# A 2x2-block form in seven products for the FFN's second matrix product, with operands passed through DRAM

## The chip, the cores and the metric

The kernel runs on one core of one Trainium2 chip. The time is the device time of one execution in microseconds; a kernel's time is the median of its runs. Engines are named as in the profile: PE (TensorE, matrix products; PEld loads its weights), DVE (VectorE), ACT (ScalarE), POOL (GpSimd), and SP (SyncE), which issues the transfers here. Each engine works through its own queue in order.

## The reference

One step of a two-layer encoder with 1024 prompt tokens and 64 sample tokens, all taken together as T = 1088 columns. Layer 0 is a Mamba-2 mixer and an FFN, layer 1 is a chunk-band attention and an FFN. What matters here is the FFN and what stands around it:

```python
def swiglu(u, w_in, w_out):
    g, up = jnp.split(u @ w_in, 2, axis=-1)
    return (jax.nn.silu(g) * up) @ w_out
...
        xp = xp + rmsnorm(mp, nw[1])
        xs = xs + rmsnorm(ms, nw[1])
        xp = xp + rmsnorm(swiglu(rmsnorm(xp, nw[2]), ffn_w_in[layer], ffn_w_out[layer]), nw[3])
        xs = xs + rmsnorm(swiglu(rmsnorm(xs, nw[2]), ffn_w_in[layer], ffn_w_out[layer]), nw[3])
```

D_MODEL is 1024 and the hidden width is 2816, which is 22 blocks of 128. All of it is float32. The two layers' FFNs have weights of their own.

## The kernel before

Activations lie transposed, features on the 128 partitions and tokens along the free dimension. A float32 product is computed in three passes of fp32r operands: every operand v is split into a high part (a copy on ACT, written as fp32r) and a low part (v minus the high part, on DVE), and a tile of the output sums high x high, high x low and low x high. A "split" below means this pair of instructions. For weights it is `Weights.part` (L302 on ACT, L303 on DVE).

The FFN's first product (`run_pair`, L1224 to L1277, matmuls L1240 to L1242 into `px`) already works on 2x2 blocks: the weights and the normed input are cut in halves along both of their axes, and seven products of block sums (`PRODS`, L330) stand in place of eight. It runs over pairs of hidden blocks t and over two token halves, b = 0 (512 tokens, two quarters of 256) and b = 1 (576 tokens, two quarters of 288). Five pairs of b = 0 are computed plainly (`plain_pairs`). Each gated hidden block is stored to DRAM (`hscr`).

The FFN's second product (L1396 to L1430, matmuls L1410 to L1412 into `po`) is plain. Three token slices (`SL`: 384, 384 and 320 columns) are the outermost loop, then 8 output tiles m, then 22 hidden blocks k, three passes each: 1584 matmuls in a layer. A task `loader` (L1291) reads the hidden blocks of a slice back from DRAM into staging tiles (`sg`) and splits them (L1303, L1304). Weights come by SP into a ring of two raw tiles (`raw`), are split into a ring of three (`hl`), and are read anew for every slice: 72 parts of 1024 or 768 columns in a layer. An output tile is copied out of PSUM by ACT; ACT squares it and POOL adds up the squares (L444).

After a slice, the task `end` norms it: `rb_steps` reduces the sums of squares over the partitions by tiny matmuls (`nst`, L451), makes the reciprocal root by ten small DVE operations (`nv`, L457 to L468), spreads it on a diagonal (`dg`, L472) and broadcasts it by a matmul (`nbp`, L480), which ACT copies to `rb` (L484). Then DVE and POOL scale the slice and add the residual (L1331, L1332). In layer 0, `end` also makes the operands of attention from the slice: splits (L1351, L1352), sums of squares (L1356, L1357), and a second `rb_steps`. Attention's weights are scaled while they are split (L312, L315), and its first products run as `unit`s (L418 to L420).

What sets the order is a recording layer. The Python code runs through the work for PE; tasks (`loader`, `end`) are generators that are spawned and take their turns when the PE stream's time (an estimate that `st.run` advances) passes the delays they yield, or when the stream waits for something that they provide (`st.wait_for`). A priority (`tc.high_priority`) moves single instructions ahead on their queue. The delays are constants at the top (`EP_W`, `ER_W`, `EQ_W`, `RB_WAIT`).

## Time and profile before

| what | us |
|---|---|
| median of 3 runs | 3074.6 (3072.13 to 3075.79) |
| profiled execution, its own time | 3078.88 |
| its span | 3077.2 |
| first products (matmuls into `px`), layers 0 and 1 | 943.0 to 1364.5, 2373.0 to 2794.8 |
| second products (matmuls into `po`), layers 0 and 1 | 1364.5 to 1636.9, 2794.8 to 3059.7 |
| hand-over to attention after layer 0's second product | from 1636.9 |
| end of the kernel after layer 1's second product | 3059.7 to 3077.2 |

In the profile, L12 is line 12 of the kernel. A window's row gives the busy time of every engine in a stretch, with the count of instructions, the granted TensorE clock, the share of the DMA engines and the rate. A group's row gives the instructions of one line and shape: count, total busy us, mean ns of one, and the idle time that its engine had just before them, with what ended most of it. A timeline's row begins with start and duration; in brackets stands the idle time before it and what ended that.

### The profile page before, as it was taken

How to read it: one execution, taken by the hardware profiler on the slowest of the kernel's cores; microseconds unless marked ns; L12 is line 12 of the kernel's file. 1: busy time of each engine (PE TensorE's matmuls, PEld its weight loads, DVE VectorE, ACT ScalarE, POOL GpSimd, SP SyncE). 2: the span in 40 equal slices, each digit the busy share in tenths (PEclk: the TensorE clock that was granted, in tenths of full speed). 3: DMA queues.
4: the chain of work that ended last, by engine and by line, in shares of the span. 5: the costliest groups of instructions: out<-in, count | busy, mean ns of one | idle time of the engine just before them, and what ended most of it. 6: DMA issues, size and time to landing. Idle time of an engine off the chain costs nothing. (4 is left out here: it accounts for less than half of the span.)

```text
span 3077.2 us, 57007 instructions
## 1 busy us (share of the span) xinstructions
PE 2974.8 (97%) x21665; PEld 2908.0 (95%) x21665; DVE 2120.1 (69%) x4582; ACT 1422.8 (46%) x2599; POOL 844.3 (27%) x969
## 2 busy tenths in 40 slices
PE   8999999999999999999999999999898999999998
PEld 8899999999999999999999899999898999999997
DVE  8988888885878544674576777767578645575544
ACT  6655555554543322344455655555553322244432
POOL 1334343421343334331231000000153334342112
PEclk9999999999999999999999999999998999999999
DMA  3333233334443222355563222222344222246654
GB/s 118 119 86 110 87 108 88 109 119 149 147 152 92 75 81 78 102 165 171 177 199 120 85 63 63 69 64 83 121 140 131 79 78 79 76 122 183 205 182 132
DMA packets 200419, 354.36 MB, mean 115 GB/s; under 512 B 21104, under 2 KB 150192, under 8 KB 200144
## 3 DMA queue, kind: packets, MB, share of 16 engines
q1 hardware_dynamic: 200080, 350.64, 37.2%
q8 instruction: 170, 2.79, 0.4%
q14 instruction: 105, 0.86, 0.1%
q0 software_dynamic: 64, 0.07, 0.0%
HBM read 283.30 MB, written 62.87 MB: 112 GB/s over the span
## 5 line engine op out<-in xcount | busy, mean ns | idle before, releaser
L418 PE MATMUL mm<-r,hl 128*128 128x384 f32 (+2 forms) x1632 | 549.0, 336 | 7.0 <-ACT r L1717 6.3
L303 DVE TENSOR_TENSOR hl<-raw,hl 128x1024 fp32r<-128x1024 f32 (+1 forms) x276 | 337.5, 1224 | 307.3 <-ACT hl L302 306.2
L420 PE MATMUL mm<-r,hl 128*128 128x384 f32 (+2 forms) x1632 | 530.5, 325 | 3.6 <-DVE hl L315 2.8
L419 PE MATMUL mm<-r,hl 128*128 128x384 f32 (+2 forms) x1632 | 529.7, 325 | 0.7 <-DVE r L1718 0.7
L302 ACT CAST hl<-raw 128x1024 fp32r<-128x1024 f32 (+1 forms) x276 | 279.2, 1012 | 277.9 <-DMA raw<-in_w_f_dram 99.8
L1241 PE MATMUL px<-r,hl 128*128 128x288 f32 (+1 forms) x1192 | 350.0, 294 | 0.0
L444 POOL TENSOR_TENSOR ssum<-ssum,sq 128x256 f32<-128x256 f32 (+3 forms) x153 | 171.1, 1120 | 576.4 <-ACT sq L443 572.9
L418 PEld LDWEIGHTS mm<-r,hl 128*128 128x128 f32 x1632 | 311.7, 191 | 8.9 <-ACT r L1717 6.5
L420 PEld LDWEIGHTS mm<-r,hl 128*128 128x128 f32 x1632 | 310.4, 190 | 5.3 <-DVE hl L315 4.2
L1240 PE MATMUL px<-r,hl 128*128 128x288 f32 x1056 | 311.2, 295 | 4.3 <-DVE u L1255 4.3
L419 PEld LDWEIGHTS mm<-r,hl 128*128 128x128 f32 x1632 | 311.6, 191 | 1.4 <-DVE r L1718 1.0
L1242 PE MATMUL px<-r,hl 128*128 128x288 f32 x1056 | 310.9, 294 | 0.0
L1242 PE MATMUL px<-rx,hl 128*128 128x256 f32 x816 | 229.2, 281 | 7.1 <-DVE hl L303 7.1
L1240 PE MATMUL px<-rx,hl 128*128 128x256 f32 x816 | 229.9, 282 | 0.1
L1241 PEld LDWEIGHTS px<-r,hl 128*128 128x128 f32 x1192 | 224.0, 188 | 0.1
L1411 PE MATMUL po<-rx,hl 128*128 128x384 f32 (+1 forms) x640 | 207.6, 324 | 0.0
L1240 PEld LDWEIGHTS px<-r,hl 128*128 128x128 f32 x1056 | 198.6, 188 | 5.4 <-DVE u L1255 5.4
L1410 PE MATMUL po<-rx,hl 128*128 128x384 f32 (+1 forms) x608 | 199.1, 327 | 0.0
L1242 PEld LDWEIGHTS px<-r,hl 128*128 128x128 f32 x1056 | 198.4, 188 | 0.0
L1412 PE MATMUL po<-rx,hl 128*128 128x384 f32 (+1 forms) x608 | 197.3, 325 | 0.2 <-DVE hl L303 0.2
L1241 PE MATMUL px<-rx,hl 128*128 128x256 f32 x680 | 190.7, 280 | 0.0
L260 POOL TENSOR_TENSOR tt<-raw 128x512 f32<-128x512 f32 x44 | 60.2, 1369 | 398.7 <-DMA raw<-in_w_f_dram 301.9
(337 smaller groups left out, 8187.9 us busy)
## 6 DMA issues: line engine op xcount, KB each, us to landing
raw<-in_w_f_dram SPq DMA_DIRECT2D x204, 512.0 KB, 3.7
raw<-in_w_in_dram SPq DMA_DIRECT2D x40, 512.0 KB, 3.7
raw<-in_w_f_dram SPq DMA_DIRECT2D x48, 384.0 KB, 3.2
sg<-hscr SPq DMA_DIRECT2D x88, 192.0 KB, 3.6
raw<-in_w_so_dram SPq DMA_DIRECT2D x32, 512.0 KB, 3.9
dm<-acd SPq DMA_DIRECT2D x64, 192.0 KB, 3.8
raw<-in_w_kv_dram SPq DMA_DIRECT2D x18, 512.0 KB, 3.7
raw<-in_w_o_dram SPq DMA_DIRECT2D x16, 512.0 KB, 3.8
```

The source lines that it names most:

```text
L302: self.nc.scalar.copy(h, v)
L303: (eng or self.eng or self.nc.vector).tensor_tensor(lo, v, h, op=ALU.subtract)
L418: PE.matmul(ps[:, :n], h_, xh, start=(first and i == 0), stop=False)
L419: PE.matmul(ps[:, :n], h_, xl, start=False, stop=False)
L420: PE.matmul(ps[:, :n], l_, xh, start=False, stop=(last and i == nk - 1))
L444: (eng or G).tensor_tensor(ssum[:, :n], ssum[:, :n], q[:, :n], op=ALU.add)
L1240: PE.matmul(ps, wh, ah[:, k, :], start=(k == 0), stop=False)
L1241: PE.matmul(ps, wh, al[:, k, :], start=False, stop=False)
L1242: PE.matmul(ps, wl, ah[:, k, :], start=False, stop=(k == 3))
L1410: PE.matmul(ps[:, :n], wh, xh, start=(k == 0), stop=False)
L1411: PE.matmul(ps[:, :n], wh, xl, start=False, stop=False)
L1412: PE.matmul(ps[:, :n], wl, xh, start=False, stop=(k == FT - 1))
```

## The change

The second product is cut as the first one: output tiles in two halves (4 tiles j each), hidden blocks in even and odd ones (11 pairs k), tokens in the two quarters of each half b. Seven products take the place of eight. The loop over products (`PHASES`) is outermost: P1, P6, P2, P7 and P5 for both halves b, then P4 and P3 for b = 0, then P4 and P3 for b = 1. Each product of a half takes 4 x 11 x 3 matmuls of 256 or 288 columns, 1848 in a layer. Its weights come in parts of 768 and 640 columns (`KIT`), read once for both halves in the shared phases and once for each half in the last four.

- The seven operands of a pair k (two of the four hidden blocks' own rows, a11 and so on, and four sums, s1 to s4) are formed in the first product (`Hidden.row`, `Hidden.sums`): four sums on DVE for each pair and half, and a store of every operand to a DRAM scratch `hop`. The first blocks of a pair wait for their partner in a lent tile of the ring R, in a stage tile, or in their own tile.
- The four weight sums (`Hidden.weights`) are formed in the first product too: 16 rounds, one in 17 of the stream's us, each with four loads into stage tiles behind a tiny POOL copy, four sums on DVE and four stores to the scratch `wt`.
- The order of the first product's pairs (`RUN`) begins with pair 5 and then has pair 4 for b = 1 alone, and ends with four pairs of b = 1 alone, where five stood at the end before.
- `loader` brings the operands back and splits them, 154 tiles of 256 or 288 columns in place of 66 of 384 or 320.
- A product is not copied out but added on DVE to accumulators (L1612), 56 additions in a layer in place of 24 copies on ACT (the first product's 8 are still copies). The additions follow the Winograd form.
- `end` runs for four quarters instead of three slices. In layer 0 quarters are put together to attention's slices (`PIECES`, L1501, with sums of squares L1506 on POOL or DVE into `tot0`, `tot1`).
- Weights may take a third raw tile, lent by the ring R. Attention's evacuations `evq` and `evv` wait for the slice's `rb`.

The core of the diff:

```diff
+WT_GAP = 17.0
...
-EP_W, ER_W, EQ_W = (9.4, 9.4, 5.0), (8.9, 8.9, 4.5), (11.0, 11.0, 11.0)
+EP_W, ER_W, EQ_W = (5.0, 5.0), (7.0, 7.0), (6.0, 6.0)
...
+KH = FT // 2
+FH = KH * P
+KORD = [*range(5, KH), *range(5)]
+KIT = (0, 6), (6, 5)
+WCH = (0, 3), (3, 3), (6, 3), (9, 2)
+RUN = [(5, (0, 1)), (4, (1,))] + [(t, (0, 1)) for t in range(6, FT)] + [(t, (1,)) for t in range(4)]
...
+PHASES = [(p_, (0, 1)) for p_ in (P1, P6, P2, P7, P5)] + [(P4, (0,)), (P3, (0,)), (P4, (1,)), (P3, (1,))]
...
-    hd_ = [dr.tile([P, FT, T], F32, name=f"hscr{i}") for i in range(2)]
+    hop_ = [dr.tile([P, 7, KH, T // 2], F32, name=f"hop{i}") for i in range(2)]
+    wt_ = [dr.tile([P, 4, 4, FH], F32, name=f"wt{i}") for i in range(2)]
...
-        for s in range(NSL):
-            for m in range(KD):
-                for k0, nk in KCH:
-                    W.plan(dict(src=[w2[m][:, k0 * P:(k0 + nk) * P]], n=nk * P))
+        for p_, _ in PHASES:
+            for j in range(4):
+                for k0, nk in KIT:
+                    if p_ in (P1, P2, P3):
+                        v = half(w2[j + 4 * (p_ == P3)], p_ != P1, k0, nk)
+                    else:
+                        v = wt[:, j, {P6: WT2, P7: WT3, P5: WT1, P4: WT4}[p_], k0 * P:(k0 + nk) * P]
+                    W.plan(dict(src=[v], n=nk * P, lend=1))
...
+        def sums(self, b, t_, c, u_):
+
+            if self.first(b, t_):
+                return
+            F, S = self.held[b, 0], self.held[b, 1]
+            q = nsb.tile([P, 384], F32, tag="sq", bufs=2, name="hs")[:, :BN[b] // 2]
+            if t_ % 2:
+                (a21, a11, a22, a12), (s3, s1, s2, s4) = (F, S, c, u_), (S, F, q, u_)
+            else:
+                (a22, a12, a21, a11), (s3, s1, s2, s4) = (F, S, c, u_), (q, c, F, S)
+            for i, d, x_, y_, op in (
+                ("s3", s3, a11, a21, ALU.subtract), ("s1", s1, a21, a22, ALU.add),
+                ("s2", s2, a22, s3, ALU.subtract), ("s4", s4, a12, s2, ALU.subtract),
+            ):
+                V.tensor_tensor(d, x_, y_, op=op)
+                self.store(b, t_, OPI[i], d)
+            self.ok.add((b, KORD.index(t_ // 2)))
...
+        def weights(self):
+
+            w2, wt = w_f2[self.layer], wt_[self.layer]
+            for j in range(4):
+                for k0, nk in WCH:
+                    b22, b12, b11, b21 = (stage[0]()[:, :nk * P] for _ in range(4))
+                    G.tensor_copy(b22[:, 0:1], self.held[1, 0][:, 0:1])
+                    for t_, m, h in ((b22, j + 4, 1), (b12, j + 4, 0), (b11, j, 0), (b21, j, 1)):
+                        nc.sync.dma_start(blocks(t_), half(w2[m], h, k0, nk))
+                    for i, d, x_, y_, op in (
+                        (WT3, b22, b22, b12, ALU.subtract), (WT1, b12, b12, b11, ALU.subtract),
+                        (WT2, b11, b22, b11, ALU.add), (WT4, b21, b21, b11, ALU.subtract),
+                    ):
+                        V.tensor_tensor(d, x_, y_, op=op)
+                        nc.sync.dma_start(wt[:, j, i, k0 * P:(k0 + nk) * P], d)
+                    yield 0, WT_GAP
...
+                    d = hid.out(b, t_, 0, x["c22"])
+                    G.tensor_tensor(d, x["p1"], x["u2"], op=ALU.mult)
+                    hid.row(b, t_, 0, d)
+            if p_ == P3:
+                hid.sums(b, t_, x["c22"], x["u3"])
...
+                        yield 0, 0, lambda: (b, k) in hid.ok and sh.room((b, k, 0), (b, k, 1))
+                        h_, l_ = (rr(sh.get((b, k, part))) for part in range(2))
+                        n = BN[b] // 2
                         t_ = stage[0]()[:, :n]
                         with tc.high_priority(LDP):
-                            nc.sync.dma_start(t_, hd[:, k, o:o + n])
+                            nc.sync.dma_start(t_, hid.hop[:, OPN[p_], k, b * 256:b * 256 + n])
                             A.copy(h_, t_)
                             V.tensor_tensor(l_, t_, h_, op=ALU.subtract)
...
+                    yq = ys[qq]
+                    for m in range(KD):
+                        uh, ul = u[s][m]
+                        ym, ss_ = yq[m // 4][:, m % 4, c:c + w_], tot[s][:, a:a + w_]
+                        with tc.high_priority(ENP[last]):
+                            A.copy(uh[:, a:a + w_], ym)
+                            V.tensor_tensor(ul[:, a:a + w_], ym, uh[:, a:a + w_], op=ALU.subtract)
+                        if m == 0:
+                            A.activation(ss_, ym, AF.Square)
+                        else:
+                            A.activation(ym, ym, AF.Square)
+                            (V if last and m % 2 else G).tensor_tensor(ss_, ss_, ym, op=ALU.add)
+                        yield 0, ES[last]
...
+                if q:
+                    s = q - 1
+                    done2.append(s)
+                    yield 0, EQ_W[last]
+                    yield from rb_steps(tot[s], SL[s][1], [], ER_W[last], rb_out[s])
+                    done2.append(("rb", s))
...
+                for i, (t_, bs) in enumerate(RUN):
+                    ends = ((0,) if t_ == FT - 1 else ()) + ((1,) if i == len(RUN) - 1 else ())
+                    run_pair(t_, W.get(), bs, ends, ops, hid, px, tmp, i == 0)
+                    if i == 3:
+                        st.spawn(hid.weights())
...
+            for p_, bs in PHASES:
+                for j in range(4):
+                    ps = {b: px.tile([P, 512], F32, tag="mm", name="po") for b in bs}
+                    for k0, nk in KIT:
                         w = W.get()
                         h, v = w["w"]
+                        for b in bs:
+                            n = BN[b] // 2
+                            for k in range(k0, k0 + nk):
+                                st.wait_for(lambda: (p_, b, k) in hl)
+                                xh, xl, sh = hl[p_, b, k]
+                                a = (k - k0) * P
+                                wh, wl = h[:, a:a + P], v[:, a:a + P]
+                                PE.matmul(ps[b][:, :n], wh, xh, start=(k == 0), stop=False)
+                                PE.matmul(ps[b][:, :n], wh, xl, start=False, stop=False)
+                                PE.matmul(ps[b][:, :n], wl, xh, start=False, stop=(k == KH - 1))
...
+                            if p_ == P1:
+                                A.copy(at("p1"), pb_)
+                            else:
+                                for d, x_ in {
+                                    P6: (("u2", "p1"),), P2: (("p1", "p1"),), P7: (("u3", "u2"),),
+                                    P5: (("c22", "u3"), ("u2", "u2")), P4: (("u3", "u3"),), P3: (("u2", "u2"),),
+                                }[p_]:
+                                    V.tensor_tensor(at(d), pb_, at(x_), op=ALU.add)
...
+                if len(bs) == 1:
+                    b = bs[0]
+                    q = 2 * b + (p_ == P3)
+                    ys[q] = (acc["p1", b], acc["u2", b]) if p_ == P3 else (acc["u3", b], acc["c22", b])
+                    st.spawn(end(q, ys[q], ss[q], more))
...
         def evq(j):
             def f(s, p_):
                 n = SL[s][1]
+                st.wait_for(lambda: ("rb", s) in done)
```

Lines move by the change: `nst` L451 to L501, `nv` L457 to L507 and following, `dg` L472 to L522, `nbp` L480 to L530, the units L418 to L468, weight splits L303 to L349 and L315 to L361, the norm steps L1331 and L1332 to L1478 and L1479, attention's splits L1352 to L1501.

PE at the hand-over from layer 0's second product to attention, before, behind the last slice: the reduction `nst` of the last slice's norm stands among units (`mm`) of attention.

```order
L419 MATMUL mm<-r,hl 128x384
L420 MATMUL mm<-r,hl 128x384
L451 MATMUL nst<-ones,ssum 128x1 x3
L418 MATMUL mm<-r,hl 128x384
L419 MATMUL mm<-r,hl 128x384
```

The broadcast `nbp` that belongs to it stands 32 rows later, again among units:

```order
L418 MATMUL mm<-r,hl 128x384
L419 MATMUL mm<-r,hl 128x384
L420 MATMUL mm<-r,hl 128x384
L480 MATMUL nbp<-dg,frac 128x320
L418 MATMUL mm<-r,hl 128x384
```

PE at the same place now, 24 units behind the last product; `tot` holds the sums for attention's first slice, `ssum` those of a quarter's own norm.

```order
L469 MATMUL mm<-r,hl 128x384
L470 MATMUL mm<-r,hl 128x384
L501 MATMUL nst<-ones,tot_16708 128x1 x3
L501 MATMUL nst<-ones,ssum 128x1 x3
L530 MATMUL nbp<-dg,frac 128x384
L468 MATMUL mm<-r,hl 128x384
L469 MATMUL mm<-r,hl 128x384
```

Two reductions and a broadcast that stood apart, with units between them, stand in direct succession.

DVE at the same place, before: behind the last weight splits of the second product (L303) come attention's weights (L315), an evacuation of attention (`vt`) and the small operations of the norm.

```order
L303 TENSOR_TENSOR hl<-raw,hl 128x1024 x2
L303 TENSOR_TENSOR hl<-raw,hl 128x768
L303 TENSOR_TENSOR hl<-raw,hl 128x1024 x2
L303 TENSOR_TENSOR hl<-raw,hl 128x768
L315 SCALAR_TENSOR_TENSOR hl<-raw,pcs,hl 128x128 x24
L1568 TENSOR_TENSOR vt<-mm,rbf 128x384
L457 TENSOR_SCALAR nv<-nst 128x3
L458 TENSOR_SCALAR nv<-nv 128x3
L461 TENSOR_TENSOR nv<-nv 128x3
L466 TENSOR_TENSOR nv<-nv 128x3
L467 SCALAR_TENSOR_TENSOR nv<-nv 128x3
L468 SCALAR_TENSOR_TENSOR nv<-nv 128x3
```

DVE now: the first row is the last addition out of PSUM (L1612); `u` and `c` are accumulators, the latter of a quarter that is being normed.

```order
L1612 TENSOR_TENSOR u_17313<-po,u_17313 128x288
L1479 TENSOR_TENSOR c_18583<-c_18583,r 128x288
L361 SCALAR_TENSOR_TENSOR hl<-raw,pcs,hl 128x128 x12
L1478 SCALAR_TENSOR_TENSOR c_18583<-c_18583,pcs,rb 128x288
L507 TENSOR_SCALAR nv<-nst 128x3 x2
L508 TENSOR_SCALAR nv<-nv 128x3
L1478 SCALAR_TENSOR_TENSOR c_18583<-c_18583,pcs,rb 128x288
L511 TENSOR_TENSOR nv<-nv 128x3
L508 TENSOR_SCALAR nv<-nv 128x3
L1479 TENSOR_TENSOR c_18583<-c_18583,r 128x288
L516 TENSOR_TENSOR nv<-nv 128x3
L511 TENSOR_TENSOR nv<-nv 128x3
```

The small operations of two norms (`x2`) now stand behind attention's weights and among the last norm steps of a quarter.

DVE within the second product, before, where the second slice is normed (L1331, L1332) while weights for the third one are split (L303):

```order
L1331 SCALAR_TENSOR_TENSOR y<-y,pcs,rb 128x384 x2
L1332 TENSOR_TENSOR y<-y,rx 128x384
L1331 SCALAR_TENSOR_TENSOR y<-y,pcs,rb 128x384 x2
L1332 TENSOR_TENSOR y<-y,r 128x384
L1331 SCALAR_TENSOR_TENSOR y<-y,pcs,rb 128x384
L303 TENSOR_TENSOR hl<-raw,hl 128x1024
L1332 TENSOR_TENSOR y<-y,r 128x384
L1331 SCALAR_TENSOR_TENSOR y<-y,pcs,rb 128x384 x3
L1332 TENSOR_TENSOR y<-y,r 128x384
L303 TENSOR_TENSOR hl<-raw,hl 128x1024
L1352 TENSOR_TENSOR r<-y,r 128x384 x3
L303 TENSOR_TENSOR hl<-raw,hl 128x768
```

DVE now, in the last two products of layer 0 (b = 1), where the first half's quarters are normed (L1478, L1479) and split for attention (L1501):

```order
L349 TENSOR_TENSOR hl<-raw,hl 128x768
L1479 TENSOR_TENSOR r<-r 128x256
L1478 SCALAR_TENSOR_TENSOR r<-r,pcs,rb 128x256
L1478 SCALAR_TENSOR_TENSOR c_18578<-c_18578,pcs,rb 128x256 x2
L1479 TENSOR_TENSOR c_18578<-c_18578,r 128x256
L349 TENSOR_TENSOR hl<-r,hl 128x640
L1612 TENSOR_TENSOR u_18152<-po,u_18152 128x288
L1478 SCALAR_TENSOR_TENSOR c_18578<-c_18578,pcs,rb 128x256 x2
L1479 TENSOR_TENSOR c_18578<-c_18578,r 128x256
L507 TENSOR_SCALAR nv<-nst 128x2
L1501 TENSOR_TENSOR r<-r 128x256
L508 TENSOR_SCALAR nv<-nv 128x2
```

Splits stood among norm steps before as well; now additions out of PSUM (L1612) and the small operations of a norm stand among them too, and four quarters are worked off within the last four products.

300 lines of the change are left out of this document (191 added, 109 removed).

## Prediction

> **What bounds the kernel now.** I read the busy shares first, then windows over the four long stretches of the two FFNs.
>
> ```profile
> span 3077.2 us, 57007 instructions
> PE 2974.8 (97%) x21665; PEld 2908.0 (95%) x21665; DVE 2120.1 (69%) x4582; ACT 1422.8 (46%) x2599; POOL 844.3 (27%) x969
> core 0: us, PE busy (x) PEld busy (x) DVE busy (x) ACT busy (x) POOL busy (x), PEclk, DMA share, GB/s
> 1364.50:1636.90 272.40, 268.58 (x1619) 266.45 (x1618) 150.40 (x213) 123.95 (x211) 56.13 (x47) 0.99 0.60 184
> 2794.80:3059.70 264.90, 264.34 (x1604) 263.04 (x1602) 124.99 (x160) 105.14 (x162) 39.18 (x32) 1.00 0.59 183
> 943.00:1364.50 421.50, 415.28 (x3279) 414.39 (x3278) 260.58 (x420) 144.12 (x235) 168.39 (x139) 0.99 0.30 93
> 1300.00:1364.00 64.00, 61.92 (x466) 61.23 (x465) 55.77 (x80) 30.55 (x51) 32.25 (x24) 1.00 0.47 146
> 2600.00:2700.00 100.00, 100.00 (x805) 100.00 (x805) 51.09 (x91) 28.43 (x47) 40.10 (x35) 1.00 0.27 81
> 1450.00:1500.00 50.00, 50.00 (x289) 49.51 (x288) 38.45 (x55) 25.93 (x47) 14.64 (x12) 1.00 0.72 232
> 1480.00:1490.00 10.00, 10.00 (x60) 10.00 (x59) 10.00 (x13) 5.16 (x10) 6.24 (x6) 1.00 0.64 207
> ```
>
> PE is busy for 97% of the span. The first two windows are the second products of layers 0 and 1, the third is layer 0's first product. In all of them PE has almost no idle time, so a product costs its matmuls times their pitch. The pitch follows the width: at 384 columns it is 50/289 = 0.173 us (1450 to 1500), and in the first product, which alternates 256 and 288 columns, 100/805 = 0.1243 us (2600 to 2700). Fewer and narrower matmuls are therefore paid in full, as long as operands arrive. The profiled execution took 3078.9 us (span 3077.2 and 1.7 around it), 4.3 above the median of 3074.6. I sum against 3078.9 and take 4.3 off at the end.
>
> **What goes.** Now 3 slices x 8 tiles x 22 blocks x 3 passes = 1584 matmuls per layer; afterwards 7 products x 2 halves x 4 tiles x 11 blocks x 3 passes = 1848, of 256 and 288 columns, the mix of the first product: 1848 x 0.1243 = 229.7 us. Against the two windows that saves 272.4 - 229.7 = 42.7 us in layer 0 and 264.9 - 229.7 = 35.2 in layer 1, together **77.9 us**. Layer 0's window holds stalls, and the matmuls behind them run slower:
>
> ```profile
> 1593.97 0.41 PE L1410 MATMUL po<-r,hl 128*128 128x320 f32 x1 [2.60 <-ACT hl L302]
> 1596.45 0.47 PE L1410 MATMUL po<-rx,hl 128*128 128x320 f32 x1
> 1596.72 0.47 PE L1411 MATMUL po<-rx,hl 128*128 128x320 f32 x1
> 1667.75 2.41 PE L451 MATMUL nst<-ones,ssum 128*128 128x1 f32 x10 [4.84 <-POOL ssum L1357]
> 3059.16 0.31 PE L1411 MATMUL po<-rx,hl 128*128 128x320 f32 x1
> 3059.31 0.31 PE L1412 MATMUL po<-rx,hl 128*128 128x320 f32 x1
> 3060.14 1.28 PE L451 MATMUL nst<-ones,ssum 128*128 128x1 f32 x10 [0.41 <-ACT ssum L1421]
> 3061.46 0.16 DVE L457 TENSOR_SCALAR nv<-nst 128x3 f32<-128x3 f32 x1 [0.77 <-PE nst L451]
> 3061.65 0.17 DVE L458 TENSOR_SCALAR nv<-nv 128x3 int32<-128x3 int32 x1
> 3063.42 0.56 DVE L472 TENSOR_TENSOR dg<-ident,nr 128x384 f32<-128x384 f32 x1
> 3064.04 1.44 PE L480 MATMUL nbp<-dg,frac 128*128 128x320 f32 x2 [2.62 <-DVE dg L472]
> ```
>
> After the wait of 2.60 us the pitch is 0.27 us (1596.45 to 1596.72) where 320 columns else take 0.15 (3059.16 to 3059.31, rounded). Ten or so such matmuls cost some 1.5 us, which I add to every longer stall.
>
> **What comes: DVE.** Durations by shape, from layer 0's second product to the end (x, total, mean ns):
>
> ```profile
> L303 DVE TENSOR_TENSOR hl<-raw,hl 128x1024 fp32r<-128x1024 f32 x135 | 172.3, 1277 | 194.0 <-ACT hl L302 193.6
> L303 DVE TENSOR_TENSOR hl<-raw,hl 128x768 fp32r<-128x768 f32 x48 | 48.9, 1020 | 57.6 <-ACT hl L302 57.6
> L315 DVE SCALAR_TENSOR_TENSOR hl<-raw,pcs,hl 128x128 fp32r<-128x128 f32 x208 | 65.7, 355 | 5.8 <-ACT hl L312 5.5
> L1331 DVE SCALAR_TENSOR_TENSOR y<-y,pcs,rb 128x384 f32<-128x384 f32 x32 | 27.2, 890 | 0.5 <-ACT rb L484 0.5
> L1304 DVE TENSOR_TENSOR r<-sg,r 128x384 fp32r<-128x384 f32 x33 | 20.4, 645 | 9.7 <-ACT r L1303 9.6
> L1352 DVE TENSOR_TENSOR r<-y,r 128x384 fp32r<-128x384 f32 x16 | 15.3, 1000 | 1.0 <-ACT r L1351 1.0
> L1173 DVE SCALAR_TENSOR_TENSOR rx<-rx,pcs,rb 128x256 f32<-128x256 f32 x16 | 11.2, 751 | 0.0
> L1185 DVE SCALAR_TENSOR_TENSOR rx<-rx,pcs,rb 128x256 f32<-128x256 f32 x16 | 7.9, 528 | 1.8 <-ACT rb L484 1.8
> L1267 DVE TENSOR_TENSOR u<-px,u 128x288 f32<-128x288 f32 x23 | 10.4, 452 | 7.3 <-PE px L1242 7.3
> L1332 DVE TENSOR_TENSOR y<-y,r 128x384 f32<-128x384 f32 x14 | 7.7, 548 | 0.0
> L444 POOL TENSOR_TENSOR ssum<-ssum,sq 128x256 f32<-128x256 f32 x28 | 29.1, 1042 | 45.2 <-ACT sq L443 44.3
> L444 POOL TENSOR_TENSOR ssum<-ssum,sq 128x288 f32<-128x288 f32 x28 | 27.4, 981 | 20.4 <-ACT sq L443 19.3
> L1273 POOL TENSOR_TENSOR c<-p,u 128x256 f32<-128x256 f32 x17 | 13.8, 810 | 0.2 <-POOL u L1269 0.2
> ```
>
> *First product.* Each layer gets 11 x 2 x 4 = 88 operand sums of 256 or 288 columns and 64 weight sums of 256 or 384. At L1332's 548 ns for 384 columns (1.43 ns a column) that is 34 + 32 us, with 152 stores and 64 loads on SP. DVE rises from 260.6 to some 327 of 421.5 us, 78%, and PE covers it: PE ran without idle in window 2600 to 2700 with DVE at 51% and POOL at 40%. Were the cover gone, all 66 us would be late. What is dense already is the end: 55.8 of 64 us (1300 to 1364). I take **2 us** a layer, with 0 and 10 as ends: ten single-half sums of about 0.4 us in the last runs, twice over.
>
> *Shared phases* (five products for both halves, 1320 x 0.1243 = 164 us of PE). DVE gets 110 operand splits (272 columns on average, at L1304's 645/384 = 1.68 ns: 50 us), 40 weight splits (20 of 768 at 1.02, 20 of 640 at about 0.87: 38) and 40 evacuations that are now sums (L1267, about 0.44: 18): 106 of 164 us. PE covers that but for waits like the 2.60 above: **2 us** a layer (0 to 5).
>
> *Layer 0's last two phases*, where each half's output is normed and handed to attention while weights are still split. The last excerpt in the section on the change shows splits (L349) queued behind norm steps (L1478) on DVE's one queue. PE needs 264 matmuls x 0.133 us (288 columns) = 35.1 us here. DVE, counted in the order between the last evacuation of P3's first half and the last of all: 14 splits, 7 of 768 and 7 of 640 columns, 7 x 1.02 + 7 x 0.87 = 13.2 (640 lies between the rows); 8 evacuations at 0.45 = 3.6; L1478, 14 of 256 and 5 of 288, 10.3 by L1185's row to 14.9 by L1173's, 12.6; L1479, 10, 4.1; L1501, 4096 columns in 24 pieces, 6.9 by L1304's to 10.7 by L1352's, 9; two chains of small operations and `dg`, 5; four of L315's kind, 1.4. Sum **49 us** against 35.1, so weights come 14 us late, less 2 for what is queued last and no weight needs: **12**, with 6 and 18 as ends (the low and high rows of L1478 and L1501).
>
> *Hand-over to attention.* PE's excerpt of the changed order shows `nst` and `nbp` with nothing between, and only 24 unit matmuls (24 x 0.173 = 4.2 us) after the last product; before, 30 stood between. Behind the last evacuation DVE holds 20 small operations at a pitch of 0.2 (4.0), 20 of L361 (L315 before) at 0.355 (7.1), two `dg` (1.1) and norm steps (some 3): 15 us, so PE waits 15 - 4 = 11, and 2 more for the slow clock: **13**, with 4 (the unhindered chain, 3060.14 to 3064.04) and 17 as ends. Two further `nst`/`nbp` pairs cost about one unhindered chain less the units between, **3 + 3** (1 to 5 each). The old stall of 4.84 goes: **-4.8**. Slow matmuls after two waits for weights: **3**.
>
> *Layer 1's end.* Nothing is handed on there; counted in the same way, DVE has about 27 of 35 us; its tail is as before (288 columns instead of 320), with one evacuation more ahead of the square. **3 us** (0 to 5).
>
> Layer 0: 42.7 - (2 + 2 + 12 + 13 + 6 - 4.8 + 3) = 9.5. Layer 1: 35.2 - (2 + 2 + 3) = 28.2. Sum 37.7: 3078.9 - 37.7 = 3041.2, and 4.3 off: **3037 us** (own range 3020 to 3056).
>
> **Rivals.** *B: the chains hide.* Only unhindered chains remain: 4 + 2 + 2 - 4.8 + 1.6, first product and shared phases 4, tail 0.5, nothing else: 9.3 of 77.9 lost, 3010 less 4.3, **3006**. For it: ACT idles half of the time, and weights have a third raw buffer. Against: 49 us in 35.
>
> *C: DMA sets the pace of the single phases.*
>
> ```profile
> raw<-in_w_f_dram SPq DMA_DIRECT2D x204, 512.0 KB, 3.7
> raw<-in_w_f_dram SPq DMA_DIRECT2D x48, 384.0 KB, 3.2
> sg<-hscr SPq DMA_DIRECT2D x88, 192.0 KB, 3.6
> ```
>
> In the last 66 us I count 11.5 MB of weights, 2 of operands, 3.3 of the residual and 2.1 of stores, 18.9 MB. The busiest row above moved 232 GB/s at a share of 0.72; at 232 it takes 81 us, 15 late per layer, at 232/0.72 = 322 it takes 59 and fits. In place of 12 and 3 the loss is up to 27 and 18 or some 22 more in all: **3059**.
>
> *R: VectorE and GpSimd take turns in layer 0's last two phases.* L1352 took 1000 ns beside GpSimd work where L1304, the same shape, took 645. POOL has 17 operations of 256 columns there at 0.81, 11 of 288 at 0.98 and 14 of 128 at about 0.4, 30 us. If turns were complete, DVE's 49 without PSUM reads and small operations (40) and these 30 make 70 us, late by 35 in place of 14: **3058**. Against it stands the dense row, 10.00 of DVE and 6.24 of POOL in 10 us, unless an instruction that waits for its turn is recorded as busy. The Trainium skill, SBUF — State Buffer, section "Who interferes with whom", states this as a rule: a VectorE instruction with two SBUF inputs and a GpSimd one that reads SBUF exclude each other for a whole instruction. By that page the sum would be 3058; the rows show slowing of that kind, and can't tell waiting from work.
>
> *D: slower, the first product.* If DVE and POOL took turns there, 260.6 + 66 + 168.4 = 495 us of work would stand in 421.5, 73 a layer: 3037 + 146 = **3183**. It decides from 19 us a layer on, which eats the 37.7. For it: today's 260.6 + 168.4 already fill the 421.5. Against: 55.8 and 32.3 busy in 64 us, 138%, with PE at 97%.
>
> *E: the change doesn't do what it says*, the pitch not falling with the width: at 0.15, as for 320 columns now, 1848 of them take 277 us, the gain turns into a loss of 5 + 12, and with the costs of 40: 3078.9 + 17 + 40 - 4.3 = **3132**, slower. The first product's row at the same widths speaks against.
>
> **How the numbers follow.** Chances: forecast 0.48, B 0.20, C 0.12, R 0.10, D 0.07, E 0.03. The range 3003 to 3066 holds B, the forecast's own range and the prices of C and R. What a measurement of this kernel can tell from no change is about 0.2%, 6 us. D and E are slower, 0.10. Of C and R, whose prices lie 15 below the old time, 0.05 falls within 0.2%. Faster: 0.85.
>
> **What would show it.** Right: the second products near 230 us plus stalls, in layer 0 waits on `hl` L348/L349 in the last 35 us, and one long wait on `dg` L522 behind L1777's products. B would show no wait over 4 us there; C waits on `raw` from DMA at a share near 1; R doubled L1501 and L1478; D idle PE between first-product matmuls. Wrong: waits elsewhere, or a first product over 430 us.

## The result, and the profile after

The changed kernel takes 3216.6 us (median, 3216.0 to 3220.3), the kernel before 3075.2 in the same session: ratio 1.0461 (95% interval 1.0443 to 1.048). It is slower by some 141 us, where 38 less were forecast.

The page's head and the windows over the four FFN products of the changed kernel, first products first, then four stretches inside the second products: one of layer 0's shared phases, layer 0's last two phases (P4 and P3 of b = 1), layer 1's P3 of b = 0, and layer 1's last two phases:

```profile
span 3214.5 us, 60252 instructions
PE 2976.2 (93%) x22195; PEld 2892.4 (90%) x22195; DVE 2338.4 (73%) x5248; ACT 1439.4 (45%) x2810; POOL 868.2 (27%) x1041
...
core 0: us, PE busy (x) PEld busy (x) DVE busy (x) ACT busy (x) POOL busy (x), PEclk, DMA share, GB/s
942.80:1442.10 499.30, 444.28 (x3280) 435.94 (x3279) 330.29 (x563) 137.64 (x236) 176.86 (x156) 0.95 0.45 139
2446.70:2942.60 495.90, 441.93 (x3280) 434.43 (x3279) 326.74 (x558) 137.40 (x234) 174.26 (x155) 0.94 0.45 140
1442.00:1692.00 250.00, 239.41 (x1871) 235.98 (x1870) 172.43 (x345) 130.54 (x297) 52.17 (x61) 0.99 0.69 202
2942.40:3192.20 249.80, 238.95 (x1872) 236.12 (x1870) 164.65 (x326) 116.75 (x243) 37.54 (x41) 0.99 0.69 202
...
1500.00:1550.00 50.00, 50.00 (x403) 50.00 (x402) 28.65 (x60) 23.91 (x52) 2.32 (x4) 1.00 0.63 179
1642.60:1692.00 49.40, 41.21 (x282) 38.83 (x281) 49.16 (x97) 29.48 (x81) 34.56 (x41) 0.97 0.69 215
...
3130.80:3149.60 18.80, 17.13 (x140) 16.28 (x139) 11.64 (x24) 8.09 (x14) 4.90 (x6) 1.00 1.01 308
3149.60:3192.20 42.60, 38.30 (x282) 37.21 (x280) 38.53 (x74) 15.27 (x27) 19.69 (x22) 1.00 0.68 205
```

The second products are shorter, as meant. The time is lost where the operands are formed: layer 0's first product grew from 421.5 to 499.3 us with the same matmuls. Idle time of PE in it rose from 6.2 (421.50 - 415.28) to 55.0 us, and the busy time by another 29.0 (444.28 against 415.28): 48.8 + 29.0 = 77.8. Some 21 of the 29.0 go with the granted clock, which is 0.95 over 499.3 us where it was 0.99 over 421.5 (25.0 - 4.2); the rest wasn't traced. By stage, with the forecast's terms beside it (first to last matmul of each stage, from the timelines):

| stage | before | after | difference | forecast |
|---|---|---|---|---|
| first product, layer 0 | 421.5 | 499.3 | +77.8 | +2 |
| first product, layer 1 | 421.5 | 495.9 | +74.4 | +2 |
| second product, layer 0 | 272.5 | 250.1 | -22.4 | -42.7 + 2 + 12 + 3 = -25.7 |
| second product, layer 1 | 264.8 | 249.8 | -15.0 | -35.2 + 2 + 3 = -30.2, with the end |
| from there to layer 1's first product, all of attention | 736.5 | 754.7 | +18.2 | 13 + 6 - 4.8 = +14.2 |
| after the last product | 17.5 | 22.3 | +4.8 | in the 3 above |
| the rest, rounding included | | | -0.5 | 0 |
| span | 3077.2 | 3214.5 | +137.3 | -37.7 |

What PE and DVE waited for there: groups by line and shape in layer 0's first product, of the kernel before and of the changed one. The last part of a row is the engine's idle time just ahead of the group and what ended it.

```profile
L1255 DVE TENSOR_TENSOR u<-px,p 128x288 f32<-128x288 f32 (+1 forms) x39 | 17.2, 440 | 66.1 <-PE px L1242 65.3 <-ACT p L1252 0.8
...
L1257 DVE TENSOR_TENSOR p<-px,p 128x288 f32<-128x288 f32 (+1 forms) x39 | 17.2, 442 | 28.5 <-PE px L1242 28.1
```

```profile
L1377 PE MATMUL px<-r,hl 128*128 128x288 f32 x528 | 162.8, 308 | 43.3 <-DVE u L1392 33.9 <-DVE p L1394 9.1 <-DVE u L1410 0.3
...
L1326 DVE TENSOR_TENSOR sg<-sg 128x384 f32<-128x384 f32 (+1 forms) x64 | 34.1, 533 | 70.3 <-DMA sg<-in_w_f_dram 69.7
...
L324 DVE TENSOR_TENSOR tt<-tt,raw 128x512 f32<-128x512 f32 x21 | 17.8, 846 | 27.3 <-POOL tt L306 27.3
L1305 DVE TENSOR_TENSOR r<-r 128x288 f32<-128x288 f32 (+1 forms) x18 | 16.7, 926 | 22.0 <-POOL r L1412 19.9 <-DMA hop<-r 2.2
L1305 DVE TENSOR_TENSOR r<-r,c 128x288 f32<-128x288 f32 (+1 forms) x17 | 16.1, 949 | 12.7 <-POOL c L1412 12.7
...
L1392 DVE TENSOR_TENSOR u<-px,p 128x288 f32<-128x288 f32 (+1 forms) x39 | 16.2, 434 | 0.0
L1394 DVE TENSOR_TENSOR p<-px,p 128x288 f32<-128x288 f32 (+1 forms) x39 | 16.8, 436 | 3.4 <-PE px L1379 3.0
```

Before, DVE's evacuations waited for PE: 65.3 and 28.1 us ahead of two of their lines. Now they wait for nothing, and PE waits for them. DVE's waits moved to the added sums: the weight sums (L1326) stood 69.7 us for their loads, and the two groups of operand sums (L1305) shown 32.6 us for GpSimd's gated product (L1412). L324, the first product's own block sums of weights, waited 27.3 us for GpSimd's part of them (L306); before it was 18.4. The timeline of the changed kernel at the end of one pair shows how a wait of DVE becomes one of PE:

```profile
1314.57 0.47 POOL L1319 COPY sg<-r 128x1 f32<-128x1 f32 x1
1315.07 1.98 SPq L1321 DMA_DIRECT2D sg<-in_w_f_dram  x4
...
1312.33 1.51 DVE L1305 TENSOR_TENSOR r<-r 128x256 f32<-128x256 f32 x1 [1.53 <-POOL r L1412]
1314.54 0.46 DVE L1305 TENSOR_TENSOR r<-r 128x288 f32<-128x288 f32 x1 [0.70 <-POOL r L1412]
1314.92 0.42 DVE L1392 TENSOR_TENSOR u<-px,p 128x256 f32<-128x256 f32 x1
1320.74 0.56 DVE L1326 TENSOR_TENSOR sg<-sg 128x384 f32<-128x384 f32 x1 [5.41 <-DMA sg<-in_w_f_dram]
1321.22 0.45 DVE L1392 TENSOR_TENSOR u<-px,p 128x288 f32<-128x288 f32 x1
...
1316.80 0.28 PE L1379 MATMUL px<-rx,hl 128*128 128x256 f32 x1
1321.72 0.61 PE L1377 MATMUL px<-r,hl 128*128 128x288 f32 x1 [4.64 <-DVE u L1392]
...
1312.26 1.30 POOL L349 TENSOR_TENSOR half<-raw,half 128x512 fp32r<-128x512 f32 x1
```

DVE reads one half's evacuation (L1392, 256 columns) at 1314.92, and the next instruction of its queue is a weight sum whose four loads SP has only just begun to issue (1315.07). It stands for 5.41 us. The other half's evacuation, 0.45 us of work, is queued behind it, and PE, whose accumulator it frees, is still for 4.64 us.

DVE's whole time in the stage, with its idle time by the engine that ended it (summed from the brackets of the timeline):

| us | stage | busy | idle for PE | ACT | POOL | DMA | other |
|---|---|---|---|---|---|---|---|
| before | 421.5 | 260.6 | 106.9 | 35.1 | 18.4 | | 0.5 with DMA |
| after | 499.3 | 330.3 | 8.5 | 24.1 | 61.9 | 72.9 | 1.6 |

69.7 more work, 72.9 and 43.5 more waits for DMA and POOL and 1.1 of the rest make 187.2. Of it 98.4 were taken from waits for PE and 11.0 from those for ACT; 77.8 were left, and the stage is that much longer.

### The profile page after: what moved, and what is told of

Read it like the earlier page. It is cut to its first block, busy times and chain, and to the rows that moved or that the text cites. A ratio compares the mean times of both kernels' runs of the same rounds, so it can differ in the third digit from the quotient of the medians.

```text
span 3214.5 us, 60252 instructions
## 1 busy us (share of the span) xinstructions
PE 2976.2 (93%) x22195; PEld 2892.4 (90%) x22195; DVE 2338.4 (73%) x5248; ACT 1439.4 (45%) x2810; POOL 868.2 (27%) x1041
## 5 line engine op out<-in xcount | busy, mean ns | idle before, releaser
L468 PE MATMUL mm<-r,hl 128*128 128x384 f32 (+2 forms) x1632 | 550.2, 337 | 7.7 <-ACT r L1926 6.5
L1377 PE MATMUL px<-r,hl 128*128 128x288 f32 x1056 | 325.4, 308 | 86.6 <-DVE u L1392 67.2
L1378 PE MATMUL px<-r,hl 128*128 128x288 f32 (+1 forms) x1192 | 360.0, 302 | 0.1
L349 DVE TENSOR_TENSOR hl<-raw,hl 128x1024 fp32r<-128x1024 f32 (+2 forms) x230 | 257.7, 1122 | 128.1 <-ACT hl L348 127.0
L494 POOL TENSOR_TENSOR ssum<-ssum,sq 128x256 f32<-128x256 f32 (+1 forms) x167 | 173.2, 1040 | 597.1 <-ACT sq L493 589.3
L1379 PE MATMUL px<-r,hl 128*128 128x288 f32 x1056 | 320.9, 304 | 0.2 <-DVE hl L349 0.2
L468 PEld LDWEIGHTS mm<-r,hl 128*128 128x128 f32 x1632 | 312.0, 191 | 10.0 <-ACT r L1926 6.7
L1377 PEld LDWEIGHTS px<-r,hl 128*128 128x128 f32 x1056 | 207.3, 196 | 94.8 <-DVE u L1392 72.0
L348 ACT CAST hl<-raw 128x1024 fp32r<-128x1024 f32 (+2 forms) x230 | 214.3, 932 | 164.7 <-PE po L1588 59.1
L1377 PE MATMUL px<-rx,hl 128*128 128x256 f32 x816 | 238.2, 292 | 11.8 <-DVE u L1392 9.3
L1379 PE MATMUL px<-rx,hl 128*128 128x256 f32 x816 | 234.6, 288 | 9.0 <-DVE hl L349 9.0
L1378 PEld LDWEIGHTS px<-r,hl 128*128 128x128 f32 x1192 | 233.8, 196 | 0.7 <-DVE r L1165 0.7
L1588 PE MATMUL po<-rx,hl 128*128 128x256 f32 (+1 forms) x704 | 204.0, 290 | 7.8 <-DVE hl L349 7.6
L1586 PE MATMUL po<-rx,hl 128*128 128x256 f32 (+1 forms) x704 | 204.0, 290 | 6.1 <-ACT r L1606 5.3
L1379 PEld LDWEIGHTS px<-r,hl 128*128 128x128 f32 x1056 | 207.7, 197 | 0.4 <-DVE hl L349 0.4
L1587 PE MATMUL po<-rx,hl 128*128 128x256 f32 (+1 forms) x704 | 202.5, 288 | 0.0
L306 POOL TENSOR_TENSOR tt<-raw 128x512 f32<-128x512 f32 x44 | 60.2, 1369 | 510.8 <-DMA raw<-in_w_f_dram 428.2
L1378 PE MATMUL px<-rx,hl 128*128 128x256 f32 x680 | 196.2, 289 | 0.0
```

Of the source, the lines that this page charges most:

```text
L348: self.nc.scalar.copy(h, v)
L349: (eng or self.eng or self.nc.vector).tensor_tensor(lo, v, h, op=ALU.subtract)
L468: PE.matmul(ps[:, :n], h_, xh, start=(first and i == 0), stop=False)
L494: (eng or G).tensor_tensor(ssum[:, :n], ssum[:, :n], q[:, :n], op=ALU.add)
L1377: PE.matmul(ps, wh, ah[:, k, :], start=(k == 0), stop=False)
L1378: PE.matmul(ps, wh, al[:, k, :], start=False, stop=False)
```

## The experiments

Four theories, named by letters below. **V**: the sums wait at the head of VectorE's queue (for loads, for GpSimd), the evacuations behind them are late, and PE stands. The expectations call it W as well, S where only the wait for GpSimd is meant, and B where it is put as a budget: added work and waits use up the time in which VectorE waited for PE (95 us at the two evacuations shown) before they cost anything. **T** (rival D of the prediction): VectorE and GpSimd exclude each other, or VectorE has too much work. **P**: the preparation of the first product's weights, which the change leaves at a raised priority behind the first pair, goes ahead of the products and evacuations that PE waits for. **Q**: SP's queue, on which the sums' stores stand, makes later loads late. All times of the stage are of layer 0's first product (before 421.5, after 499.3), layer 1's in brackets where it adds something.

**One kind of sum alone, or none.**

`e2_no_wsums` forms no weight sums; every phase reads plain weights.

```diff
-                        v = wt[:, j, {P6: WT2, P7: WT3, P5: WT1, P4: WT4}[p_], k0 * P:(k0 + nk) * P]
+                    v = half(w2[j + 4 * (p_ == P3)], p_ != P1, k0, nk)
...
-                        st.spawn(hid.weights())
```

> Leaves the weight sums out, with their loads and stores; every product of the second product reads blocks of w2 as they are in their place. W: first products 420 to 430, kernel 3060 to 3080, and little better than with the late sums. T: VectorE loses 34 of 330 us in a first product, PE gets back about that much, first products near 460, kernel near 3150.

`e3_no_hsums` stores a plain block where an operand sum belongs:

```diff
-                V.tensor_tensor(d, x_, y_, op=op)
-                self.store(b, t_, OPI[i], d)
+                self.store(b, t_, OPI[i], x_)
```

> Leaves the operand sums of the first product out (88 on VectorE in a layer) and stores one of each sum's two inputs in its place, so that the transfers stay. W: the waits at the weight sums stay, first products fall by at most 20 each, kernel 3175 to 3216. T: VectorE loses some 54 of 330 us, first products near 440, kernel near 3110. A rival S, by which the sums' own waits for GpSimd's product (35 us of VectorE's idle time in a layer) are what PE waits for, expects about 460 and 3140.

`e7_no_sums` has both edits.

> Leaves both kinds of sums out: blocks of w2 as they are in place of weight sums, and one input of each operand sum stored in its place. Theory B (VectorE's queue has a budget: before the change it stood 95 us of a first product at the first two evacuations of a pair, waiting for PE, and what is added to it in work and in waits at its head comes out of these 95 first): nothing is added, first products 421 to 428, the kernel 3055 to 3075, so that even free sums would leave only some 10 us of gain. Had the second product itself nothing to lose, the 78 us of the sum would show: 2997 to 3010.

| | time, ratio to before | stage | DVE busy | idle for PE | POOL | DMA |
|---|---|---|---|---|---|---|
| e2, operand sums only | 3094.0, 1.0058 (1.0038 to 1.0079) | 438.6 | 303.3 | 37.2 | 51.4 | 5.2 |
| e3, weight sums only | 3112.3, 1.0118 (1.0098 to 1.0138) | 452.2 | 283.2 | 35.8 | 24.7 | 40.1 |
| e7, neither | 3064.7, 0.9965 (0.9955 to 0.9974) | 423.0 | 252.3 | 105.4 | 18.1 | under 1 |

Neither e2 nor e3 came out as V had it (e2 at 420 to 430, e3 at most 20 below 499). e2's stage lies between V's and T's 460, and e3's time is near T's 3110, so these two alone don't decide between V and T. e7 lies within B's range. The operand sums alone cost 17.1 us of the stage, the weight sums alone 30.7, both 77.8. Together they are more than the sum of the two: each alone leaves 36 or 37 of the 106.9 us in which DVE waits for PE unused, both leave 8.5. All loss goes with the sums and the loads and stores of the weight sums: without them, but with the store of every operand, the stage is at 423.0, and its row is nearly the old one.

```profile
940.70:1363.70 423.00, 415.75 (x3280) 414.61 (x3279) 252.33 (x416) 140.10 (x234) 166.74 (x139) 0.99 0.35 109
```

e7 also gives the value of everything else: with sums and their weights' transfers for nothing the change would gain 0.35%, not the forecast's 1.2%.

**Where the sums stand.**

`e1_late_wsums` puts 8.5 us of the stream between a round's loads and its sums.

```diff
+                    yield 0, WT_LAG
...
-                    yield 0, WT_GAP
+                    yield 0, WT_GAP - WT_LAG
```

> Everything is computed; only the place of the weight sums moves: the four sums of a round are issued 8.5 of the stream's us after its four loads, not at once. Theory W (VectorE's queue stands still at the first weight sum until its loads land, about 5 us in each of 16 rounds, and the evacuations behind it leave PE without a PSUM tile): the first products fall from 499 and 496 us to 422 to 435 each and the kernel to 3070 to 3100. Theory T (VectorE and GpSimd have too much to do side by side, the added sums as such cost): the sums are as many as before, so the first products stay over 480 and the kernel over 3185.

A miss: 3222.8 us, 1.0475 (1.0458 to 1.0493), stage 503.2. DVE still waited 73.2 us for DMA. The program was written later, but the sums came out at the same place of the queue, so this run says nothing against V; it says that a delay is no means to move them.

`e4_tied_wsums` ties the sums to data instead. A round's loads go out after a pair's last product, and its sums are recorded at P5 of the next pair, the first of them multiplied by a 1 that is made from that pair's evacuated tile, so that it can't be put earlier. The rounds begin behind the first pair and not the fourth, and a round's four stores stand behind all of its sums.

```diff
+            V.tensor_scalar(one, v[:, 0:1], 0.0, 1.0, op0=ALU.mult, op1=ALU.add)
+            V.scalar_tensor_tensor(b22, b22, one, b12, op0=ALU.mult, op1=ALU.subtract)
...
+            if p_ == P5 and b == bs[-1]:
+                hid.late(x["c22"])
```

> Everything is computed. The late weight sums did not move on VectorE's queue (the scheduler put them back behind the second evacuation of a pair), so here the first sum of a round reads a column made from the next pair's fifth product, which ties it to that place, half a pair behind its loads. Theory W (the wait of VectorE's queue for the loads is what costs): VectorE no longer idles 70 us at the weight sums, the first products take 435 to 455 us each and the kernel 3085 to 3125. Theory T (the number of VectorE's operations is what costs): as many as before, first products over 480, kernel over 3185.

3132.2 us, 1.0187 (1.0168 to 1.0207), stage 459.0: just above V's ranges and far from T's. Over half of the loss is gone, with the same loads, sums and stores and 16 tiny operations more. Timeline, window and groups (first product of layer 0):

```profile
1152.19 1.98 SPq L1325 DMA_DIRECT2D sg<-in_w_f_dram  x4
...
1162.59 0.14 DVE L1335 TENSOR_SCALAR one<-c 128x1 f32<-128x1 f32 x1
1162.77 0.62 DVE L1336 SCALAR_TENSOR_TENSOR sg<-sg,one 128x384 f32<-128x384 f32 x1
...
942.20:1401.20 459.00, 427.51 (x3279) 421.32 (x3279) 346.32 (x579) 137.59 (x235) 181.06 (x156) 0.98 0.48 152
...
L1336 DVE SCALAR_TENSOR_TENSOR sg<-sg,one 128x384 f32<-128x384 f32 (+1 forms) x16 | 10.4, 650 | 0.5
L1390 PE MATMUL px<-rx,hl 128*128 128x256 f32 x408 | 117.6, 288 | 16.5 <-DVE u L1405 16.5
L1390 PE MATMUL px<-r,hl 128*128 128x288 f32 x528 | 157.2, 298 | 10.2 <-DVE u L1405 10.2
```

The chain of sums begins 10.4 us after the first load was issued, and its head waits 0.5 us in all 16 rounds together. DVE is busy for 346.3 us, 16 more than in the changed kernel, in 40.3 us less. That is against T: more work, less loss. DVE's waits for DMA fell from 72.9 to 15.7, of which 13.5 are an evacuation's (L1411) for the store of an operand. Those for POOL didn't fall: 64.9, with 40.9 at L324 and 24.1 at the operand sums. Of PE's 31.5 us of idle time 26.7 are now waits for the evacuation L1405, which stands right behind the operand sums in DVE's queue.

`e8_tied_no_hsums` is e4 with e3's edit.

> The tied weight sums, computed; the operand sums are left out as in the run without them. B: some 45 us added to VectorE against a budget of 95, first products 421 to 433, kernel 3058 to 3090. If each sum cost its own time (T), 45 a layer: first products near 466, kernel near 3150.

3079.3 us, 1.002 (1.0009 to 1.003), stage 435.3 (432.5), just above B's range in layer 0, within it in layer 1, and far from T's 466. Taken strictly the budget fails: 13.8 us are lost while DVE still waits 63.5 us for PE. Tied, the weight sums cost 13.8 us where they cost 30.7 in e3. The 37.5 that e4 still loses are thus for the greater part the operand sums' own, or those of both together.

**The priority.** `e5_pri0` sets it back after every pair, and `e6_tied_pri0` does so in e4.

```diff
+                    W.pri = 0
```

> Everything is computed. The preparation of the first product's weights loses its raised priority behind the first pair, as it stood before the change. Theory P (the raised preparation on GpSimd and VectorE delays the products and evacuations that PE waits for): first products 440 to 480, kernel 3100 to 3180. W and T: no change beyond 20 us either way.

> Both edits together. W with P: first products below 440, kernel 3070 to 3100. W alone: as with the tied sums, within 15 us. T: over 3185.

3219.5, 1.0472 (1.0451 to 1.0493), and 3133.3, 1.0189 (1.0172 to 1.0206): nothing, beside 1.0461 and 1.0187. P falls.

**Work without waits.** In the kernel before, additions of 384 columns are put on VectorE that read a constant and wait for nothing; nobody uses them. `e9_extra6` has six a pair, `e10_extra12` twelve.

```diff
+            if p_ in (P1, P2, P5) and b == bs[-1]:
+                for _ in range(2):
+                    q = nsb.tile([P, 384], F32, tag="sq", bufs=2, name="extra").rearrange("p (a c) -> p a c", c=P)
+                    o = ones.unsqueeze(1).to_broadcast([P, 3, P])
+                    V.tensor_tensor(q, o, o, op=ALU.add)
```

> The kernel before the change with six idle additions of 384 columns on VectorE (0.56 us each, results unused, no wait for another engine) in each pair of a first product: 74 us a layer. B: within the budget, first products 421 to 430, kernel 3075 to 3095. T: 74 a layer, kernel near 3220.

> The same with twelve in a pair: 148 us a layer. B: about 50 over the budget, first products 455 to 480, kernel 3140 to 3195. T: 148 a layer, kernel near 3370. If work without waits costs nothing at all (only waits do), no change: 3075.

e9: 3144.8 us, 1.0231 (1.0211 to 1.0252), stage 447.3, a miss. The additions weren't spread: free of inputs, they came in the first five or six pairs, up to eight in a row ahead of an evacuation, and the stage lost 25.8 us there. e10: 3182.0 us, 1.0352 (1.0332 to 1.0373), stage 467.2, within B's range, and both first products began some 8 to 10 us late besides (24 of layer 0's additions ran ahead of its first product). Timeline of e9, then window and group of e10:

```profile
1063.70 5.74 DVE L1279 TENSOR_TENSOR extra<-ones 128x384 f32<-128x384 f32 x8
```

```profile
952.70:1419.90 467.20, 431.54 (x3279) 425.23 (x3278) 395.29 (x658) 142.35 (x236) 179.82 (x139) 0.97 0.27 84
...
L1279 DVE TENSOR_TENSOR extra<-ones 128x384 f32<-128x384 f32 x241 | 148.4, 662 | 0.0
```

With 395.3 us of work DVE holds 134.7 more than before, nearly twice what the change added, and loses 45.7 us, where the change lost 77.8. So work without waits isn't free either: it cost a third of its length here, and how much of the changed kernel's 77.8 is its work's own isn't settled by this run. It is against T as a question of amount, as T had 3370 us, with the reserve that the extras read one small tile twice, where a sum reads two full ones.

**The queues.** `e11_wsums_pool` gives the weight sums to GpSimd, and `e12_pool_pri0` does so with e5's edit. `e13_stores_pool` leaves the sums on VectorE and issues their stores from GpSimd's queue instead of SP's; `e14_wsums_stores_pool` moves both.

```diff
-                        V.tensor_tensor(d, x_, y_, op=op)
+                        G.tensor_tensor(d, x_, y_, op=op)
...
-                        nc.sync.dma_start(wt[:, j, i, k0 * P:(k0 + nk) * P], d)
+                        G.dma_start(wt[:, j, i, k0 * P:(k0 + nk) * P], d)
```

> Everything is computed. The weight sums move from VectorE's queue to GpSimd's, right behind their gate; there they stand where GpSimd waited for the next pair's weights anyway. Theory W (what costs is at the head of which queue the wait for the loads stands): as good as without weight sums, first products 435 to 450, kernel 3088 to 3115. Theory T (the operations as such, VectorE and GpSimd taking turns): GpSimd's sums are slower than VectorE's, first products over 470, kernel over 3150.

> The same with the first product's weight preparation at its old priority behind the first pair. If GpSimd's order (preparation ahead of the products that the operand sums wait for) makes up part of what is left, 5 to 20 us less than with the sums on GpSimd alone; if not, within 6 us of it.

> The changed kernel, everything computed, with the stores of the weight sums issued by GpSimd and not by SP. Theory Q (SP's queue: the stores stand ahead of the load of the next pair's weights and wait for the sums, so that these weights come late): first products fall to 440 to 470, kernel 3100 to 3160. Theory V (VectorE's queue, where the sums wait for their loads ahead of the evacuations): first products stay at 480 to 500, kernel 3185 to 3230.

> Weight sums and their stores both on GpSimd, so that neither VectorE nor SP waits for them. Q: SP's wait was what made the sums on GpSimd slower than on VectorE (523 us), first products 435 to 460, kernel 3090 to 3140. V alone: the sums had left VectorE in that run already and it gained nothing, so something else holds it: first products over 500, kernel over 3220.

| | time, ratio | stage |
|---|---|---|
| e11, sums on GpSimd | 3259.2, 1.0603 (1.0585 to 1.0621) | 519.1 |
| e12, the same, priority back | 3261.2, 1.0608 (1.059 to 1.0625) | 523.2 |
| e13, stores from GpSimd | 3215.0, 1.0454 (1.0401 to 1.0506) | 499.4 |
| e14, both | 3237.3, 1.0526 (1.0475 to 1.0577) | 509.8 |

e11 missed: it was slower than the changed kernel, not faster. e12 lies within 6 us of it, as expected if the priority plays no part. The timeline of e11 shows that the wait only changed its queue:

```profile
1156.85 5.26 POOL L1326 TENSOR_TENSOR sg<-sg 128x384 f32<-128x384 f32 x4 [6.88 <-DMA sg<-in_w_f_dram]
...
1166.37 1.31 POOL L306 TENSOR_TENSOR tt<-raw 128x512 f32<-128x512 f32 x1 [4.26 <-DMA raw<-in_w_f_dram]
...
1167.71 0.69 DVE L324 TENSOR_TENSOR tt<-tt,raw 128x512 f32<-128x512 f32 x1 [8.27 <-POOL tt L306]
```

Now GpSimd stands 6.88 us for the loads, then sums for 5.26. The first product's own block sum of weights (L306) is queued behind, and DVE waits 8.27 us for it (L324). Its raw weights came late too, as SP issued the sums' four stores ahead of them, which left Q open. e13 tests Q: with the stores off SP, DVE still waits for the loads, and the stage is 499.4 against 499.3, within V's range. Q falls as the main cause of the changed kernel's loss. A small part isn't excluded, as GpSimd's queue now waits for the sums instead: DVE's waits for GpSimd at L324 are 27.7 us there, as in the changed kernel (27.3).

```profile
1148.19 0.56 DVE L1326 TENSOR_TENSOR sg<-sg 128x384 f32<-128x384 f32 x1 [5.18 <-DMA sg<-in_w_f_dram]
```

e14 has neither SP's stores nor DVE's sums, and is still at 509.8, as V said: the loads hold GpSimd's queue, then the sums and their stores do, with L306 and L324 behind.

No kernel that computes the whole reference was faster than the one before. The best that has the change is e4, at 1.0187.

## Why the prediction was wrong

**The failed step** is the first product: "DVE rises from 260.6 to some 327 of 421.5 us, 78%, and PE covers it", priced at 2 us a layer with an upper end of 10. The sum of work came out (330.3 busy), in part by luck: the sums added 78.0 us to the 252.3 of e7 and not 66, while the rest of DVE's work fell by 8.3. The conclusion was wrong. A share of 78% says how much DVE has to do, not that it may do it when it likes. Its queue runs in order, so an added instruction costs the wait for its inputs as well as its duration. Those waits were never priced: 69.7 us for loads that were issued just ahead of the sums, and 43.5 more for GpSimd. The first can be worked out from four issues on SP and a landing, for which the changed kernel's page has a row (the prediction had quoted 3.6 us for loads of this size, and didn't use it here):

```profile
sg<-in_w_f_dram SPq DMA_DIRECT2D x96, 192.0 KB, 4.2
```

SP takes 1.98 us for the four issues, so the last goes out 1.5 us after the first, and 4.2 later it has landed: 5.7, as the sum at 1320.74 (5.67 after 1315.07). Sixteen such waits are 91 us; 69.7 were seen at the weight sums, which is less: four rounds load only 128 KB each time, and DVE has other things to do for part of a wait. That these waits, and not the work, make about half of the loss is shown by e4 (same sums, few such waits, 40.3 of 77.8 us back). What is left in e4 stands for the most part behind the operand sums (26.7 of 31.5 us). Whether their wait for GpSimd or their own length makes it isn't shown: no run formed them later.

The prediction's price for a lost cover was in the same unit: "Were the cover gone, all 66 us would be late". 77.8 were late: the waits come on top of the work.

**Rival D** forecast the size (73 a layer, measured 77.8 and 74.4) and the sign (idle PE between first-product matmuls), but not the mechanism, so that its number came out by chance: e4 with more DVE work lost half as much, and e10 with twice the added work lost 45.7. Turns are seen in single instructions. In the timeline above an operand sum of 256 columns took 1.51 us beside GpSimd's L349 (1.30), and one of 288 columns 0.46 beside a copy of one column; the two groups of L1305 have means of 926 and 949 ns. The 78 operand sums within the window came to 57 us, where the forecast had 34 for all 88 (30 for 78).

The Trainium skill, SBUF — State Buffer, section "Who interferes with whom", says that a VectorE instruction with two SBUF inputs and a GpSimd one that reads SBUF hold each other up for a whole instruction; these two rows agree with it, and the evacuations, which read PSUM and stay at 434 to 436 ns, do as well. Longer instructions are some 27 us here, not the 78.

**The pitch and the gain** held. In the window from 1500 to 1550 there are 403 matmuls in 50.00 us, 0.1241 each, against the forecast 0.1243; rival E falls.

**Layer 0's last two phases** held: they took 49.4 us (1642.6 to 1692.0), DVE was busy for 49.16 of them, where 49 were forecast, and PE's waits there are for `hl` L349 (8.1 us). They took 14.3 us more than the 35.1 that PE needs, where 12 were forecast, so rival B falls, and so does R, which had 70 us there. The whole second product took 20.4 us over the 229.7 of its matmuls, where 2 + 12 + 3 were forecast.

**The hand-over** held in kind, and with all of attention behind it the row is 4.0 us larger than 14.2. PE's waits in it, from the timeline, are three of middle size instead of one long one:

```profile
1696.34 0.69 PE L470 MATMUL mm<-r,hl 128*128 128x384 f32 x1 [2.46 <-DVE hl L361]
...
1706.43 1.62 PE L530 MATMUL nbp<-dg,frac 128*128 128x384 f32 x2 [4.77 <-DVE nr L518]
...
1716.82 1.01 PE L501 MATMUL nst<-ones,tot 128*128 128x1 f32 x4 [4.11 <-POOL tot L1506]
```

**Layer 1's end** was mis-sized: 2 + 3 us were forecast over 229.7, and 20.1 came, with 4.8 more in the tail. The last two phases took 42.6 us (3149.6 to 3192.2) for PE's 35.1. The prediction counted "about 27 of 35 us" of DVE there; DVE was busy for 38.53, and PE's waits are again for `hl` L349 (4.3 us), so 7.5 us were lost as in layer 0, without attention's operands. Another 5.5 were lost in P1, which took 38.3 us for 32.8 (2942.4 to 2980.7), with a wait of 3.64 at 2964.72 for a copy out of PSUM (L1606). That copy stood on ACT's queue behind operand splits (L1456) that had waited 2.40 us for their loads, which is V on another engine. Most of the other 7 fell in P4 and P3 of b = 0. There the timeline shows weights that come late from DMA:

```profile
3129.08 0.37 SPq L260 DMA_DIRECT2D r<-in_w_f_dram  x1
...
3133.13 0.84 ACT L348 CAST hl<-r 128x768 fp32r<-128x768 f32 x1 [2.54 <-DMA r<-in_w_f_dram]
```

The load took 4.05 us from issue to the split (3133.13 - 3129.08), where the prediction's row had 3.2 for 384 KB, and the DMA engines are at a share of 1.01 with 308 GB/s (3130.8 to 3149.6). That is rival C's sign, but not its size: the whole phase has 1.67 us of idle PE, and in the last two phases, where C had its price, the share is 0.68. What a faster load would give there no run tried; it stays open. Without the first products' 152.2 us the changed kernel would be at 3064.4, which is where e7 came out (3064.7): the forecast of 3037 was too low by some 27 us even with the sums at no cost, most of it in layer 1's second product and tail.

## What to carry to other kernels

Before work is put on an engine because it has idle time, ask what each added instruction will wait for when it reaches the head of the queue, and who is queued behind: count the waits with the work, and compare the sum with the engine's own waits for the bottleneck (here 106.9 us), not with its free share. Some is lost before these waits are used up (13.8 us in e8). Issue the loads for such work well ahead of it (10.4 us in e4, where a round's loads needed 5.7), and tie their users to something that happens later; moving them to another queue moved the wait along. Two additions can cost more together than one by one (77.8 us here against 17.1 and 30.7).
